# FFN down projections as seven products of sums of halves, on one Trainium2 core

## The chip, the cores and the metric

One core of a Trainium2 chip (trn2) runs the whole program. The metric is the device time of one execution in microseconds, as the median of several runs. The engines are called PE (TensorE), DVE (VectorE), ACT (ScalarE), POOL (GpSimd) and SP (SyncE, which here issues the loads).

## The reference

The reference applies two transformer layers and then a second block to x of 512 tokens and 1024 channels. The change is in the feed-forward part (FFN) of the two layers, and in where the second block's modulation vector is computed:

```python
def first_block(x, norm1, w_in, ..., norm2, w_up, w_down, final_norm):
    for l in range(DEPTH):                      # DEPTH = 2
        h = rms_norm(x, norm1[l])
        ...                                     # four kinds of attention, w_out
        h2 = rms_norm(x, norm2[l])
        x = x + jnp.square(jax.nn.relu(h2 @ w_up[l])) @ w_down[l]   # 1024 -> 4096 -> 1024
    return rms_norm(x, final_norm)

def second_block(x, c, norm_g, w_ada, b_ada, ...):
        mod = c @ w_ada[l] + b_ada[l]           # 1 x 1024 by 1024 x 3072
        shift, scale, gate = jnp.split(mod, 3, axis=-1)
        ...
```

## The kernel before

All matmuls are fp32 made of three products: each operand is split into a rounded part hi and a residue lo, and `mm3` (L159 to L161) adds hi·hi, hi·lo and lo·hi in one PSUM bank. Weights come through `send` (L118, a load of 512 KB into a ring `raw` of two buffers), `make` (L129: ACT copies to `whi`, L142, and DVE or POOL subtracts to `wlo`, L143, in rings of four) and `weights`, which makes two chunks more than are in use. `plan` lists the chunks in the order of use. The FFN's lo parts are made on DVE (`lo_engine`).

The FFN of a layer (`ffn`) runs over 8 column groups c of 512 hidden units. In each, four up tiles n (128 hidden units by 512 tokens, 24 matmuls each, here called U0 to U3) are computed by `feature_proj` into the two PSUM banks `acc`; ACT takes relu (L849) and the square's hi part (L850), POOL the square (L851), DVE its lo part (L852). Then the down projection takes the four tiles against four chunks of w_down: 8 PSUM tiles (4 token tiles by 2 halves of the columns, in `acc` and `sc` by turns) of 12 matmuls each, 96 in all, and DVE adds each to x (L869). A group has thus 96 + 96 matmuls of 128x512.

In groups 1 to 6 each up tile is followed by a piece of other work: in layer 0 a row block of w_ada_2 (a further load of 512 KB through the ring `raw`, which DVE multiplies by c and adds up, L952 and L954, with three small reductions on PE), in layer 1 a copy of bias rows for the second block (`bias_copy`). `bias_tables` stands ahead of group 5 of layer 0. The tile framework keeps the order of each engine's queue and adds the waits; a buffer of a ring is written again once its last reader is done.

Of the kernel before, what the change touches and what calls it, by code (L numbers as in the profile page):

```python
# [57 lines left out]
class Kern:  # L58
    def __init__(self, ctx, tc, t):
# [19 lines left out]
        self.raws, self.prepped = {}, {}  # L79
# [38 lines left out]
    def send(self):  # L118
        ap = self.plan[self.sent]
        kt, cols = ap.shape[1], ap.shape[2]  # L120
        raw = self.wp.tile([P, 1024], F32, tag="raw", name=self.name("raw"), bufs=RAWS)
        v = raw[:, : kt * cols].rearrange("p (k c) -> p k c", k=kt)
        self.nc.sync.dma_start(v, ap)
        self.raws[self.sent] = raw
        self.sent += 1

    def make(self):
        n = self.made
        while self.sent < min(len(self.plan), n + 3):  # L129
# [284 lines left out]

    def plan_layer(self, l):
# [14 lines left out]
        for what in ORDER:  # L430
# [20 lines left out]
            else:  # L451
                out("abcd".index(what))
        for c in range(8):
            for n in range(4):
                a = c * HALF + n * P
                plan.append(ch(t["w_up"][l, :, a : a + P]))
                if l == 0 and 4 * c + n in range(4, 28):
                    part, k = divmod(4 * c + n - 4, KD)
                    self.whole.add(len(self.plan) + len(plan))
                    plan.append(  # L460
                        ch(t["w_ada_2"][0, k * P : (k + 1) * P, part * D : (part + 1) * D])
                    )
            for half in range(2):
                for k in range(2):
                    a = c * HALF + k * 256
                    plan.append(
                        ch(t["w_down"][l, a : a + 256, half * HALF : (half + 1) * HALF])
                    )
# [362 lines left out]
    def ffn(self, l):  # L831
        nc = self.nc
        hT = self.norm_to_hT(self.row(self.t["norm2"][l]))
        for c in range(8):
            if l == 0 and c == 5:
                self.bias_tables()
            acts, ready = [], []
            for n in range(4):
                if c == 0 and n == 0:
                    ready = self.first_tiles(hT, self.weights(2))  # L840
                    self.lo_engine = nc.vector
                if ready:
# [10 lines left out]
                acts.append(a)  # L853
                if 4 * c + n in range(4, 28):
                    if l == 0:
                        self.modulation(*divmod(4 * c + n - 4, KD))
                    else:
                        self.bias_copy(4 * c + n - 4)

            def group(b, half, ws):  # L860
                out = self.psum(("acc", "sc")[b % 2])
                tok = slice(b * P, (b + 1) * P)
                for n, a in enumerate(acts):
                    w = ws[n // 2]
                    self.mm3(
                        out, (a[:, 0, tok], a[:, 1, tok]), (w[0][:, n % 2], w[1][:, n % 2]), n == 0, n == 3
                    )
                xs = self.x[:, b, half * HALF : (half + 1) * HALF]
                nc.vector.tensor_tensor(xs, out, xs, ALU.add)  # L869

            if c == 7:
                self.lo_engine = nc.gpsimd
                ws = self.weights(4)
                for b in range(NB):
                    for half in range(2):
                        group(b, half, ws[2 * half : 2 * half + 2])
            else:
                for half in range(2):
                    ws = self.weights(2)
                    for b in range(NB):  # L880
                        group(b, half, ws)

    def first(self):

        tc, t = self.tc, self.t
        with ExitStack() as es:
# [4 lines left out]
            for l in range(2):  # L891
# [4 lines left out]
                with ExitStack() as e2:  # L896
                    self.fp = e2.enter_context(tc.tile_pool(name=f"ffn{l}", bufs=1))
                    self.ffn(l)
                    if l == 0:
                        g = self.ffn_row(t["norm1"][1])  # L900
                        hT = self.norm_to_hT(g)
# [564 lines left out]
```

## Time and profile before

| | |
|---|---|
| median of 3 runs | 1921.62 us (1919.59 to 1922.48) |
| the profiled execution | 1929.24 us, its span 1927.1 us |
| granted PE clock over the span | 0.98 of full speed |
| busy share of the span | PE 95%, DVE 61%, ACT 44%, POOL 33% |
| FFN of layer 0 in the trace | about 322 to 686 us |
| FFN of layer 1 in the trace | about 1003 to 1348 us |

The span is the time from the first to the last instruction in one profiled execution, which here was longer than the median of the others; durations in the rows below are of this execution. A row of a timeline gives start, length, engine, line and operation, with the tile written and those read; "x2" joins two like operations in a row.

### The profile page before, as it was taken

The numbers are of one execution on the slowest core, as the hardware profiler recorded it, in microseconds if no ns is written. First come the engines' busy times: TensorE is split into PE (matmuls) and PEld (weight loads), VectorE is DVE, ScalarE is ACT, GpSimd is POOL, SyncE is SP. The second block draws the span as 40 slices with busy tenths as digits, with TensorE's granted clock in tenths as the row PEclk, the third lists the DMA queues.
The fourth block names the chain that finished last, engine by engine and source line by source line (L and its number), as shares of the span: only waits on it lengthen the run. The fifth ranks groups of instructions, "written<-read, shape, count | busy, mean of one in ns | idle before, by whom it ended". The sixth has DMA issues, their size and how long they took to land.

```text
span 1927.1 us, 25712 instructions
## 1 busy us (share of the span) xinstructions
PE 1825.6 (95%) x9414; PEld 1524.6 (79%) x9414; DVE 1172.1 (61%) x2376; ACT 850.6 (44%) x1842; POOL 628.5 (33%) x425
## 2 busy tenths in 40 slices
PE   7899998999999998999989999999798999999898
PEld 6788877888877887888768888888677887877677
DVE  5899666555545358997664443333748544559675
ACT  5656775332322246556753333322434343534323
POOL 3334343111111233343331111112346444433454
PEclk9999999999999999999999999999899999999999
DMA  4222112454465322211132333332332332322242
GB/s 152 67 83 61 45 48 80 131 153 143 134 180 158 94 57 67 79 46 54 55 98 83 101 92 97 99 99 87 98 101 64 95 99 66 88 61 78 66 148 98
DMA packets 220652, 178.51 MB, mean 93 GB/s; under 512 B 14735, under 2 KB 191279, under 8 KB 220527
## 3 DMA queue, kind: packets, MB, share of 16 engines
q1 hardware_dynamic: 220526, 176.88, 30.9%
q8 instruction: 74, 1.21, 0.3%
q14 instruction: 52, 0.42, 0.1%
HBM read 172.50 MB, written 8.03 MB: 94 GB/s over the span
## 4 chain that ended last, share of the span: by engine, by line
PE 77%; DVE 13%; DMA 4%; ACT 2%; issue 2%; POOL 1%; SPq 0%; ACTq 0%; DVEq 0%; POOLq 0%
PE acc L159 19%; PE acc L160 19%; PE acc L161 19%; PE sc L159 5%; PE sc L160 4%; PE sc L161 4%; PE tp L371 2%; DVE p L1213 1%; PE pv L302 1%; PE pv L303 1%; DVE b L1053 1%; DMA raw<-in_w_in_dram 1%; DMA nrow<-neg 1%; POOL wlo L143 1%; DVE dsa L568 1%
## 5 line engine op out<-in xcount | busy, mean ns | idle before, releaser
L142 ACT ACTIVATE whi<-raw 128x1024 fp32r<-128x1024 f32 (+6 forms) x288 | 289.4, 1005 | 620.4 <-PE acc L160 237.7
L143 POOL TENSOR_TENSOR wlo<-raw,whi 128x1024 fp32r<-128x1024 f32 (+7 forms) x172 | 377.3, 2200 | 445.7 <-ACT whi L142 411.3
L159 PE MATMUL acc<-hTh,whi 128*128 128x512 f32 (+1 forms) x1128 | 438.0, 390 | 12.2 <-DVE kz L167 4.6
L160 PE MATMUL acc<-hTl,whi 128*128 128x512 f32 (+1 forms) x1128 | 434.2, 385 | 2.5 <-DVE hTl L167 2.5
L161 PE MATMUL acc<-hTh,wlo 128*128 128x512 f32 (+1 forms) x1128 | 433.4, 385 | 0.0
L851 POOL TENSOR_TENSOR tmp<-tmp 128x512 f32<-128x512 f32 x64 | 103.0, 1610 | 567.9 <-ACT tmp L849 567.8
L159 PEld LDWEIGHTS acc<-hTh,whi 128*128 128x128 f32 x1128 | 214.9, 191 | 57.4 <-issue 7.0
L143 DVE TENSOR_TENSOR wlo<-raw,whi 128x1024 fp32r<-128x1024 f32 x116 | 142.8, 1231 | 176.5 <-ACT whi L142 176.5
L160 PEld LDWEIGHTS acc<-hTl,whi 128*128 128x128 f32 x1128 | 215.2, 191 | 41.6 <-DVE hTl L167 3.5
L161 PEld LDWEIGHTS acc<-hTh,wlo 128*128 128x128 f32 x1128 | 215.0, 191 | 40.2
L159 PE MATMUL acc<-whi,hTh 128*128 128x256 f32 (+3 forms) x512 | 158.5, 311 | 10.8 <-DVE t L280 5.3
L160 PE MATMUL acc<-wlo,hTh 128*128 128x256 f32 (+3 forms) x512 | 156.3, 306 | 1.4 <-POOL wlo L143 1.4
L161 PE MATMUL acc<-whi,hTl 128*128 128x256 f32 (+3 forms) x512 | 157.6, 308 | 0.1
L159 PEld LDWEIGHTS acc<-whi,hTh 128*128 128x128 f32 x512 | 99.8, 196 | 16.4 <-issue 4.8
L160 PEld LDWEIGHTS acc<-wlo,hTh 128*128 128x128 f32 x512 | 100.5, 196 | 4.5 <-POOL wlo L143 2.2
L159 PE MATMUL acc<-whi,act 128*128 128x512 f32 x256 | 99.6, 395 | 4.5 <-DVE x L869 4.3
L161 PEld LDWEIGHTS acc<-whi,hTl 128*128 128x128 f32 x512 | 100.1, 196 | 3.8 <-issue 1.9
L166 ACT ACTIVATE pt<-tp 128x512 fp32r<-128x512 f32 (+3 forms) x128 | 63.2, 513 | 89.3 <-PE tp L371 37.3
L160 PE MATMUL acc<-wlo,act 128*128 128x512 f32 x256 | 100.7, 393 | 0.0
L159 PE MATMUL sc<-whi,act 128*128 128x512 f32 x256 | 99.7, 389 | 0.0
L160 PE MATMUL sc<-wlo,act 128*128 128x512 f32 x256 | 99.7, 389 | 0.0
L161 PE MATMUL sc<-whi,act 128*128 128x512 f32 x256 | 99.3, 389 | 0.0
(333 smaller groups left out, 3591.7 us busy)
## 6 DMA issues: line engine op xcount, KB each, us to landing
raw<-in_w_in_dram SPq DMA_DIRECT2D x92, 512.0 KB, 4.0
raw<-in_w_up_dram SPq DMA_DIRECT2D x64, 512.0 KB, 4.1
raw<-in_w_down_dram SPq DMA_DIRECT2D x64, 512.0 KB, 3.5
raw<-in_w_out_dram SPq DMA_DIRECT2D x24, 512.0 KB, 3.4
raw<-in_w_ada_dram SPq DMA_DIRECT2D x24, 512.0 KB, 4.2
raw<-in_w_in_dram SPq DMA_DIRECT2D x8, 416.0 KB, 5.4
x<-in_x_dram SPq DMA_DIRECT2D x4, 512.0 KB
nrow<-neg SPq DMA_DIRECT2D x8, 256.0 KB, 4.2
```

What stands on the lines that cost most here:

```text
L142: self.nc.scalar.activation(hi, raw, AF.Copy)
L143: self.lo_engine.tensor_tensor(lo, raw, f(hi), ALU.subtract)
L159: mm(out, lhsT[0], rhs[0], start=first, stop=False)
L160: mm(out, lhsT[0], rhs[1], start=False, stop=False)
L161: mm(out, lhsT[1], rhs[0], start=False, stop=last)
L166: self.nc.scalar.activation(hi, src, AF.Copy)
L302: mm(out, both, th[0], start=first, stop=False)
L303: mm(out[0:64], v[:, j, x, 0], th[1], start=False, stop=False)
L371: nc.tensor.transpose(pt[:, at : at + P], hd["p"][:, src : src + P], self.ident)
L568: nc.vector.match_replace(out=a, in_to_replace=m8, in_values=a, imm_value=TAKEN)
L851: nc.gpsimd.tensor_tensor(r[:, S:], r[:, :S], r[:, :S], ALU.mult)
L1053: nc.vector.reciprocal(dst, dst)
```

## The change

Groups 0 to 4 of layer 0 and 0 to 6 of layer 1 (`SEVEN = (5, 7)`), 12 of 16, compute the down projection as a product of 2 x 2 blocks: A are the halves of the hidden tile (tokens by hidden units), B the four chunks of w_down, and seven products M1 to M7 of sums of blocks give the result. Each product has 2 token tiles by 2 blocks of 128 hidden units by 3 = 12 matmuls, 84 in all.

- Five of the seven weight operands are sums of two chunks: POOL makes them (L194, 128x1024, into the scratch ring `tmp` of three), ACT and DVE split them as before (L207, L208). The chunks are held in a ring `rawd` of five.
- The sums of hidden halves are made by POOL (L927, L933, L934 of 256 columns, L937 of 512), and each operand is split by ACT and DVE (`put`, L917 and L918). The square is now taken by DVE from PSUM (L981).
- M1 to M5 are added up over the groups in SBUF (L958, on DVE; ACT copies in group 0), and after the last seven-product group are added to x, M1 to M4 by POOL (L963, L964), M5 by DVE. M6 and M7 go to x at once (L952).
- Products of a group are spread: M3 and M6 after its own U2 and U3, M4 and M7, M1 and M2, and M5 after U0, U1 and U2 of the next group. The other groups stay as they were, but for the square.
- The 24 modulation rows stand two by two in groups 5 to 7 of layer 0. `bias_tables` moves to group 0 of layer 1, and the rows for the next norm are loaded ahead of the end of the FFN.

The diff, cut to its core:

```diff
+MADE = {
+    "M1": ("B11", "B22", ALU.add, "A11+A22"),
+    "M2": ("B11", None, None, "A21+A22"),
+    "M3": ("B12", "B22", ALU.subtract, "A11"),
+    "M4": ("B21", "B11", ALU.subtract, "A22"),
+    "M5": ("B22", None, None, "A11+A12"),
+    "M6": ("B11", "B12", ALU.add, "A21-A11"),
+    "M7": ("B21", "B22", ALU.add, "A12-A22"),
+}
...
+SEVEN = (5, 7)
+
+def after(l, c, n):
+    late = (("B21", "M4", "M7"), ("M1", "M2"), ("M5",), ())[n] if 0 < c <= SEVEN[l] else ()
+    early = ((), (), ("B12", "B22", "M3"), ("B11", "M6"))[n] if c < SEVEN[l] else ()
+    return late + early
...
+            _, one, two, op = e
+            raw, kt, cols = self.held[one], 2, HALF
+            if two:
+                both = self.scratch()
+                self.nc.gpsimd.tensor_tensor(both, raw, self.held[two], op)
+                raw = both
+            engine = self.nc.vector
...
+    def rows_of(self, l, c, n):
+        return [divmod(8 * (c - 5) + 2 * n + i, KD) for i in range(2)] if l == 0 and c >= 5 else []
...
+        def put(a, src):
+            nc.scalar.activation(a[:, 0], src, AF.Copy)
+            nc.vector.tensor_tensor(a[:, 1], src, f(a[:, 0]), ALU.subtract)
+
+        def hidden(c, n, s, sq):
+            g = nc.gpsimd.tensor_tensor
+            j = n % 2
+            if n < 2:
+                put(operand(c, ["A11"], j), s[:, :256])
+                t = self.half()[:, :256]
+                g(t, s[:, 256:], s[:, :256], ALU.subtract)
+                put(operand(c, ["A21-A11"], j), t)
+                return
+            s0 = sq[j]
+            put(operand(c, ["A22"], j), s[:, 256:])
+            t = self.half()
+            g(t[:, :256], s[:, :256], s[:, 256:], ALU.subtract)
+            g(t[:, 256:], s0[:, :256], s[:, 256:], ALU.add)
+            put(operand(c, ["A12-A22", "A11+A22"], j, "a4", S), t)
+            t = self.half()
+            g(t, s0, s, ALU.add)
+            put(operand(c, ["A11+A12", "A21+A22"], j, "a4", S), t)
+
+        def product(c, m):
+            (w,) = self.weights()
+            for t in range(2):
+                tok = slice(t * P, (t + 1) * P)
+                out = self.psum(("acc", "sc")[t])
+                for j in range(2):
+                    a = parts[c, MADE[m][3], j]
+                    self.mm3(out, (a[:, 0, tok], a[:, 1, tok]), (w[0][:, j], w[1][:, j]), j == 0, j == 1)
...
-                r = self.scratch()
-                nc.scalar.activation(r[:, :S], pj, AF.Relu)
-                nc.scalar.activation(a[:, 0], r[:, :S], AF.Square)
-                nc.gpsimd.tensor_tensor(r[:, S:], r[:, :S], r[:, :S], ALU.mult)
-                nc.vector.tensor_tensor(a[:, 1], r[:, S:], f(a[:, 0]), ALU.subtract)
+                    r = self.half()
+                    nc.scalar.activation(r, pj, AF.Relu)
+                    q = self.st.tile([P, S], F32, tag="sq", name=self.name("sq"), bufs=4)
+                    nc.vector.tensor_tensor(q, r, pj, ALU.mult)
+                    if c < SEVEN[l]:
+                        sq.append(q)
+                        hidden(c, n, q, sq)
...
+                    for part, k in self.rows_of(l, c, n):
+                        self.modulation(part, k)
+                    if l == 1 and c == 0 and n == 1:
+                        self.bias_tables()
...
```

The order of DVE's queue before, in layer 1, from the third residue of a group's weights to its down projection; `wlo` are residues of weights, `act` those of hidden tiles, `x` the evictions:

```order
L852 TENSOR_TENSOR act_1985_10253<-tmp_1986_10254,act_1985_10253 128x512
L852 TENSOR_TENSOR act_1987_10259<-tmp_1988_10260,act_1987_10259 128x512
L143 TENSOR_TENSOR wlo_2003_10342<-raw_1989_10265,whi_2002_10341 128x1024
L852 TENSOR_TENSOR act_1993_10296<-tmp_1994_10297,act_1993_10296 128x512
L143 TENSOR_TENSOR wlo_2006_10348<-raw_1995_10302,whi_2005_10347 128x1024
L852 TENSOR_TENSOR act_1999_10333<-tmp_2000_10334,act_1999_10333 128x512
L869 TENSOR_TENSOR x_84<-acc_2007_10351,x_84 128x512
L869 TENSOR_TENSOR x_84<-sc_2008_10365,x_84 128x512
L143 TENSOR_TENSOR wlo_2013_10410<-raw_2001_10339,whi_2012_10409 128x1024
L869 TENSOR_TENSOR x_84<-acc_2009_10379,x_84 128x512
L869 TENSOR_TENSOR x_84<-sc_2010_10393,x_84 128x512
L143 TENSOR_TENSOR wlo_2016_10416<-raw_2004_10345,whi_2015_10415 128x1024
```

DVE had eight weight residues, four hidden residues and eight evictions in a group, each reading what ACT, POOL or PE had left, in this order.

The order of DVE's queue in the changed kernel, in layer 1 from the square of U2 of group 3 to that of U3. `wlo_2372` belongs to U0 of the next group, `wlo_2384` to M4, `wlo_2389` to M7 (ahead of the fence stands `wlo_2368`, of M6); `sq_2354` and `sq_2375` are the squares of U2 and U3, `a2` and `a4` the operands made of hidden sums:

```order
L981 TENSOR_TENSOR sq_2354_11327<-t2_2353_11325,acc_2352_11300 128x512
L208 TENSOR_TENSOR wlo_2372_11391<-raw_2364_11364,whi_2371_11390 128x1024
L958 TENSOR_TENSOR M3_2208_10689<-sc_2370_11382,M3_2208_10689 128x512
L918 TENSOR_TENSOR a2_2355_11329<-sq_2354_11327,a2_2355_11329 128x256
L952 TENSOR_TENSOR x_84<-sc_2386_11454,x_84 128x512
L958 TENSOR_TENSOR M3_2206_10680<-acc_2369_11374,M3_2206_10680 128x512
L208 TENSOR_TENSOR wlo_2384_11443<-tmp_2382_11440,whi_2383_11442 128x1024
L918 TENSOR_TENSOR a4_2357_11335<-t2_2356_11332,a4_2357_11335 128x512
L918 TENSOR_TENSOR a4_2359_11340<-t2_2358_11338,a4_2359_11340 128x512
L208 TENSOR_TENSOR wlo_2389_11465<-tmp_2387_11462,whi_2388_11464 128x1024
L981 TENSOR_TENSOR sq_2375_11421<-t2_2374_11419,acc_2373_11394 128x512
```

The square, which frees the PSUM bank of an up tile, now stands behind residues of weight sums and of hidden sums, which read what POOL made.

The same queue, on to the square of U0 of the next group (`sq_2392`, read from `acc_2390`); `wlo_2397` belongs to U1, `wlo_2403` to M1, and `acc_2398` is the first tile of M4:

```order
L208 TENSOR_TENSOR wlo_2397_11507<-raw_2381_11438,whi_2396_11506 128x1024
L918 TENSOR_TENSOR a2_2376_11423<-sq_2375_11421,a2_2376_11423 128x256
L918 TENSOR_TENSOR a4_2378_11429<-t2_2377_11426,a4_2378_11429 128x512
L918 TENSOR_TENSOR a4_2380_11434<-t2_2379_11432,a4_2380_11434 128x512
L208 TENSOR_TENSOR wlo_2403_11531<-tmp_2401_11528,whi_2402_11530 128x1024
L958 TENSOR_TENSOR M4_2237_10817<-acc_2398_11510,M4_2237_10817 128x512
L981 TENSOR_TENSOR sq_2392_11495<-t2_2391_11493,acc_2390_11468 128x512
```

The square of U0 stands behind the residue of M1's weights and those of U3's three operands.

POOL's queue before holds only squares of hidden tiles in the FFN of layer 1 (L851), four in a group. In the changed kernel it goes as follows from the sum for M1 (`tmp_2401`) past U2 and U3 to the operands of U3; `tmp_2426` and `tmp_2443` are the sums for M3 and M6 of the next group:

```order
L194 TENSOR_TENSOR tmp_2401_11528<-rawd_2348_11292,rawd_2342_11268 128x1024
L933 TENSOR_TENSOR t2_2356_11332<-sq_2354_11327 128x256
L934 TENSOR_TENSOR t2_2356_11332<-sq_2315_11149,sq_2354_11327 128x256
L937 TENSOR_TENSOR t2_2358_11338<-sq_2315_11149,sq_2354_11327 128x512
L194 TENSOR_TENSOR tmp_2426_11640<-rawd_2414_11592,rawd_2419_11614 128x1024
L194 TENSOR_TENSOR tmp_2443_11714<-rawd_2425_11638,rawd_2414_11592 128x1024
L933 TENSOR_TENSOR t2_2377_11426<-sq_2375_11421 128x256
L934 TENSOR_TENSOR t2_2377_11426<-sq_2333_11235,sq_2375_11421 128x256
L937 TENSOR_TENSOR t2_2379_11432<-sq_2333_11235,sq_2375_11421 128x512
```

POOL's rows went from four to thirteen in a group, five of them of 128x1024, and each reads held chunks or squares that DVE makes.

The order of PE's queue in the changed kernel, between U3 and U0 of the next group; `sc_2399` belongs to M4, `sc_2405` to M7, `acc_2390` to U0, `acc_2385` to M6:

```order
L226 MATMUL acc_2385_11446<-whi_2367_11370,a2_2336_11242 128x512
L225 MATMUL sc_2399_11518<-wlo_2384_11443,a2_2355_11329 128x512
L226 MATMUL sc_2399_11518<-whi_2383_11442,a2_2355_11329 128x512
L224 MATMUL sc_2405_11542<-whi_2388_11464,a4_2357_11335 128x512
L225 MATMUL sc_2405_11542<-wlo_2389_11465,a4_2357_11335 128x512
L226 MATMUL sc_2405_11542<-whi_2388_11464,a4_2357_11335 128x512
L224 MATMUL acc_2390_11468<-hTh_2134_10336,whi_2371_11390 128x512
```

Matmuls of M4 and M7 now stand ahead of U0, so that U0 begins behind `wlo_2384` and `wlo_2389`. The tiles `acc` take their two banks by turns: `acc_2390` (U0) that of `acc_2373` (U3), and after `acc_2398` (M4) the second tile of M7, `acc_2404`, that of `acc_2390`.

## Rows read from the trace of the kernel before

**Rows 1.** The page: span; part 1: busy us, share of span, instructions by engine.
```profile
span 1927.1 us, 25712 instructions
...
PE 1825.6 (95%) x9414; PEld 1524.6 (79%) x9414; DVE 1172.1 (61%) x2376; ACT 850.6 (44%) x1842; POOL 628.5 (33%) x425
```

**Rows 2.** Windows, layer 1's FFN: busy us (instructions) by engine, granted clock.
```profile
1050.00:1093.00 43.00, 43.00 (x191) 35.63 (x190) 17.01 (x20) 12.96 (x16) 6.39 (x4) 1.00 0.32 95
```

**Rows 3.** Timeline of PE: first matmul of two groups of layer 1.
```profile
1054.47 0.39 PE L159 MATMUL acc<-hTh,whi 128*128 128x512 f32 x1
...
1097.99 0.39 PE L159 MATMUL acc<-hTh,whi 128*128 128x512 f32 x1
```

**Rows 4.** Timelines, layer 0's FFN; in brackets idle time before and its releaser.
```profile
550.12 0.47 PE L159 MATMUL acc<-hTh,whi 128*128 128x512 f32 x1 [0.85 <-DVE tb L991]
...
587.26 0.79 PE L159 MATMUL acc<-whi,act 128*128 128x512 f32 x1 [4.25 <-DVE x L869]
...
585.32 1.28 DVE L954 SCALAR_TENSOR_TENSOR ada<-raw,cvec,ada 128x1024 f32<-128x1024 f32 x1 [5.50 <-DMA raw<-in_w_ada_dram]
586.52 0.68 DVE L869 TENSOR_TENSOR x<-acc,x 128x512 f32<-128x512 f32 x1
```

**Rows 5.** Groups by form, 1050 to 1093: count, busy us, mean ns.
```profile
L142 ACT ACTIVATE whi<-raw 128x1024 fp32r<-128x1024 f32 x8 | 8.5, 1062 | 30.4 <-PE acc L160 14.3 <-PE sc L161 10.2 <-PE acc L161 6.0
...
L851 POOL TENSOR_TENSOR tmp<-tmp 128x512 f32<-128x512 f32 x4 | 6.4, 1596 | 37.5 <-ACT tmp L849 37.5
```

**Rows 6.** Timeline of DVE: three operations in a row.
```profile
587.72 1.21 DVE L143 TENSOR_TENSOR wlo<-raw,whi 128x1024 fp32r<-128x1024 f32 x1
588.85 0.68 DVE L869 TENSOR_TENSOR x<-acc,x 128x512 f32<-128x512 f32 x1
589.45 0.68 DVE L869 TENSOR_TENSOR x<-sc,x 128x512 f32<-128x512 f32 x1
```

**Rows 7.** Timelines of PE, ACT and DVE at an up tile's end.
```profile
431.31 0.39 PE L160 MATMUL acc<-hTl,whi 128*128 128x512 f32 x1
...
431.73 1.06 ACT L142 ACTIVATE whi<-raw 128x1024 fp32r<-128x1024 f32 x1 [2.23 <-PE acc L160]
432.70 0.58 ACT L849 ACTIVATE tmp<-acc 128x512 f32<-128x512 f32 x1
...
432.82 1.23 DVE L143 TENSOR_TENSOR wlo<-raw,whi 128x1024 fp32r<-128x1024 f32 x1 [1.57 <-ACT whi L142]
```

**Rows 8.** Timelines of POOL and DVE at three places where both work.
```profile
1357.83 5.28 POOL L143 TENSOR_TENSOR wlo<-raw,whi 128x1024 fp32r<-128x1024 f32 x2 [3.61 <-ACT whi L142]
...
1360.83 2.83 DVE L926 TENSOR_TENSOR nh<-x,row 128x512 f32<-128x512 f32 x1
...
1364.25 0.67 DVE L926 TENSOR_TENSOR nh<-x,row 128x512 f32<-128x512 f32 x1
...
315.43 4.66 POOL L143 TENSOR_TENSOR wlo<-raw,whi 128x1024 fp32r<-128x1024 f32 x2 [6.94 <-ACT whi L142]
...
317.72 0.68 DVE L412 TENSOR_TENSOR x<-sc,x 128x512 f32<-128x512 f32 x1
...
338.63 3.58 POOL L851 TENSOR_TENSOR tmp<-tmp 128x512 f32<-128x512 f32 x2 [18.54 <-ACT tmp L849]
...
339.53 1.77 DVE L143 TENSOR_TENSOR wlo<-raw,whi 128x1024 fp32r<-128x1024 f32 x1 [0.21 <-ACT whi L142]
```

**Rows 9.** Groups by form on POOL over the span.
```profile
L386 POOL TENSOR_TENSOR mix<-total,mix 64x512 fp32r<-64x512 f32 x32 | 41.6, 1300 | 67.1 <-ACT mix L385 66.4
...
L281 POOL TENSOR_TENSOR t<-t,t 128x256 f32<-128x256 f32 x24 | 18.4, 769 | 56.3 <-DVE t L280 42.7 <-DVE sa L335 5.8 <-PE tp L371 5.7
```

**Rows 10.** DMA issues: count, KB, median us from issue to landing.
```profile
raw<-in_w_up_dram SPq DMA_DIRECT2D x64, 512.0 KB, 4.1
...
raw<-in_w_ada_dram SPq DMA_DIRECT2D x24, 512.0 KB, 4.2
```

More of the change, by code (lines that the diff above doesn't have):

```diff
@@ L129, in make @@
         while self.sent < min(len(self.plan), n + 3):
-            self.send()
-        ap = self.plan[n]
+            if not self.send():
+                break
+        e = self.plan[n]
         self.made += 1
-        raw = self.raws.pop(n)
-        if n in self.whole:
-            self.prepped[n] = raw
+        if isinstance(e, tuple) and e[0] == "hold":
+            self.held[e[1]] = self.raws.pop(n)
             return
-        kt, cols = ap.shape[1], ap.shape[2]
+        self.ready_made += 1
+        engine = self.lo_engine
+        if isinstance(e, tuple):
+            _, one, two, op = e
[5 more added lines that the diff above has]
+            engine = self.nc.vector
+        else:
+            raw = self.raws.pop(n)
+            if n in self.whole:
+                self.prepped[self.ready_made - 1] = raw
+                return
+            kt, cols = e.shape[1], e.shape[2]
         m = kt * cols
@@ L452, in plan_layer, with up, down @@
                 out("abcd".index(what))
+        def up(c, n):
+            a = c * HALF + n * P
+            plan.append(ch(t["w_up"][l, :, a : a + P]))
+            for part, k in self.rows_of(l, c, n):
+                self.whole.add(len(self.plan) + len(plan))
+                plan.append(ch(t["w_ada_2"][0, k * P : (k + 1) * P, part * D : (part + 1) * D]))
+        def down(c, k, half):
+            a = c * HALF + k * 256
+            return ch(t["w_down"][l, a : a + 256, half * HALF : (half + 1) * HALF])
         for c in range(8):
             for n in range(4):
[L455 to L468, printed above, removed]
+                up(c, n)
+                for what in after(l, c, n):
+                    if what in PART:
+                        plan.append(("hold", what, down(c - (what == "B21"), *PART[what])))
+                    else:
+                        plan.append(("mix",) + MADE[what][:3])
+            if c >= SEVEN[l]:
+                plan += [down(c, k, half) for half in range(2) for k in range(2)]
         return plan
@@ new lines, in ffn, with operand @@
+        parts, sums = {}, {}
+        def operand(c, key, j, tag="a2", cols=256):
+            a = self.st.tile([P, 2, cols], F32R, tag=tag, name=self.name(tag), bufs=8 if tag == "a2" else 6)
+            for x in range(0, cols, 256):
+                parts[c, key[x // 256], j] = a[:, :, x : x + 256]
+            return a
+        def put(a, src):
[9 more added lines that the diff above has]
+                put(operand(c, ["A21-A11"], j), t)
+                return
+            s0 = sq[j]
[7 more added lines that the diff above has]
+            put(operand(c, ["A11+A12", "A21+A22"], j, "a4", S), t)
@@ L883, in first, with next_rows @@
+        self.st = None
+    def next_rows(self, l):
+        if l == 0:
+            self.rows = [self.row(self.t["norm1"][1])]
+        else:
+            self.rows = [self.ffn_row(r) for r in (self.t["final_norm"], self.mod[1], self.mod[0])]
     def first(self):
@@ L899, in first @@
                     if l == 0:
[L900 to L901 removed]
+                        hT = self.norm_to_hT(*self.rows)
                     else:
```

163 lines of the change are left out of this document (101 added, 62 removed).

## The prediction

> **What bounds the kernel now.** I read the share of each engine first: TensorE (PE) is busy 95% of the 1927.1 us span [rows 1], so a saving counts only where PE works without waiting. Then the windows: in a stretch of layer 1's FFN of 43.00 us, PE is busy 43.00, VectorE (DVE) 17.01, ScalarE (ACT) 12.96, GpSimd (POOL) 6.39, at a granted clock of 1.00, that is 2.4 GHz [rows 2]. Two groups start at 1054.47 and 1097.99 [rows 3]: 43.52 us for 192 products of 128x512, or 226.7 ns each. The FFN is PE's; the other engines have more than half their time free. Only two waits of PE stand out there, 0.85 us after the bias tables and 4.25 us where DVE's evictions were queued behind a modulation row that had itself waited 5.50 us for its load [rows 4]. Any product less is worth 226.7 ns as long as nothing else comes late. So the question is whether DVE, ACT and POOL can feed the new order.
>
> **What it removes.** A seven-product group has 84 down matmuls instead of 96. 12 x 12 groups x 226.7 ns = 32.6 us off PE. The 4.25 us wait goes with the modulation rows, which leave groups 1 to 6 [rows 4]; the 0.85 us moves along with the tables into layer 1 and is counted at nothing, since the same evictions wait for the same tables.
>
> **What it adds.** I take a frame, from the end of tile U2 of one group to that of the next (steady frames: 4 in layer 0, 6 in layer 1; and one at each end of the run of seven-product groups). PE has 180 products, 40.80 us. DVE has 11 weight residues (1.13 us from one start to the next), 14 evictions, 4 squares and 4 residues of 512 (0.60 each), and 6 residues of 256, for which I take 0.33, a straight line through 1.13 and 0.60 [rows 6]: 12.4 + 13.2 + 2.0 = 27.6 us. POOL has five weight sums at 2.33 (a pair took 4.66 [rows 8]), six sums of 256 at 0.77 and two of 512 at 1.30 [rows 9]: 18.9 us. ACT grows by 128x1024 copies of 1.06 [rows 5] and stays under 30 us. Each engine alone fits into 40.80. The price lies in how two of them meet.
>
> **DVE and POOL take turns.** POOL's pair that began at 1357.83 ended at 1363.11; a DVE operation with two SBUF operands that began at 1360.83 took 2.83 us, to 1363.66, where the same line took 0.67 once POOL was idle. But an eviction from PSUM took its usual 0.68 at 317.72, in the middle of a POOL pair that ran from 315.43 to 320.09. In the FFN it is there today: a weight residue took 1.77 us beside POOL's squares at 338.63 instead of 1.21 [rows 6, 8]. So I let a POOL operation and a DVE operation with two SBUF operands exclude each other for their whole length, and evictions and squares (one PSUM operand) run beside either. The Trainium skill has this as a rule that speaks against the change: "SBUF — State Buffer", section "SBUF: two separate sides", calls the shared port pair "an exclusive lock, not a bandwidth split", which the loser waits for during the whole instruction; the rows above agree. Exclusive work in a frame: 11 x 1.13 + 6 x 0.33 + 4 x 0.60 = 16.8 on DVE and 18.9 on POOL, 35.7 of 40.8 us. That fits on average; but it is a chain, since each waits for the other, for ACT, and for buffers that PE frees. Without the exclusion the sum would be the first rival's.
>
> **Chain A**, with t = 0 at the end of U2, names as in the fences above. The copy of M6's weights waits for a buffer that U2's products read (as 431.73 waits for 431.31, with the residue at 432.82 right behind [rows 7]): copy to 1.06, residue to 2.19. It frees the buffer of M1's weight sum on POOL: 2.33 to 4.66. Then in turns: residue of U0's weights to 5.79, POOL 256 to 6.56, DVE 256 to 6.89, POOL 256 to 7.66, POOL 512 to 8.96, residue of M4 to 10.09, DVE 512 to 10.69, POOL's sum for the next M3 (its buffer freed by M4's residue) to 13.02, DVE 512 to 13.62, residue of M7 to 14.75, square of U3 to 15.44. U0 takes U3's PSUM bank, so it can start at 15.5. PE alone would be there after 60 products, 13.60. Stall 1.9 us.
>
> **Chain B** goes on: POOL's sum for the next M6 (buffer freed by M7's residue) 14.85 to 17.18, residue of U1 18.31, POOL 256 19.08, DVE 256 19.41, POOL 256 20.18, POOL 512 21.48, two DVE 512 to 22.7. ACT, in its order, copies M1's weights at 22.1 to 23.1 (the buffer is U0's, whose products end at 20.9) and U0's relu behind it to 23.7, as at 431.73 and 432.70 [rows 7]; residue of M1 24.2, an eviction 24.8, square of U0 25.5. M7's second tile takes U0's bank and was due at 15.5 + 5.44 + 2.72 = 23.6. Stall 2.0 us. The rest of the frame (48 products of M1, M2, M5 and U1, U2) has slack, since only two POOL sums lie there.
>
> Period: 40.80 + 3.9 = 44.7 us against 43.52, 1.2 longer than before.
>
> **The ends of the run and the modulation.** In the frame from group 4 to 5 of layer 0, POOL adds four finished sums to x (1.30 each) in place of one weight sum, and DVE has two modulation rows of 1.2 (585.32 to 586.52 [rows 4]): A becomes 15.5 + 5.2 - 2.33 + 2.4 = 20.8, a stall of 7.2. B there: 2.0, 1.1 for a row ahead in DVE's order, and 2.7 for a row whose load is late, chosen midway between nothing and 4.2 + 1.28 [rows 4, 10]: 5.8. From 6 to 7 of layer 1 three such additions replace a sum: A 1.9 + 3.9 - 2.33 = 3.5, B 2.0.
> Groups 6 and 7 of layer 0 now send 16 loads each through a ring of two buffers. A weight chunk holds its buffer 4.1 + 1.06 + 1.23 = 6.4 us, a modulation row 4.2 + 1.28 = 5.5 [rows 4, 5, 7, 10]: (8 x 6.4 + 8 x 5.5)/2 = 47.6 us against 43.5. Group 5, 57 us long with 60 late products (43.5 + 13.6), lets the ring run ahead. Two groups x 4.1, half of it covered: +4, bounds 0 and 9. Nothing on POOL collides there, for it is idle but for the additions to x.
>
> **Sum.** -32.6 - 4.25; layer 0: A 4 x 1.9 + 7.2, B 4 x 2.0 + 5.8 = +28.6; layer 1: A 6 x 1.9 + 3.5, B 6 x 2.0 + 2.0 = +28.9; ring +4. Together **+24.7 us**. The profiled execution, 1929.24 with a span of 1927.1, becomes 1953.9 and 1951.8. The median of the runs, 1921.62, lies 7.6 lower, so I forecast **1946 us**. The measured runs lie 2.9 apart; 0.2% is 3.8 us and about what a measurement can tell from no change.
>
> **Rivals.**
> *The exclusion falls into slack (faster).* If POOL's operations land while DVE waits for ACT or PE anyway, chain B has only ACT's order left: U0 ends at 13.60 + 5.44 = 19.04, copy of M1 20.1, residue 21.2, eviction 21.8, square 22.5, against 21.76: 0.8, and 0.2 for A. 12 frames x 1.0 + 2 for the ends: -32.6 - 4.25 + 14 = -22.9, **1899 us**; with no stall at all 1885. For it: POOL's squares of 1.60 us today delay no product [rows 2, 5]. Against it: 35.7 of 40.8 us exclude each other. It decides where a steady frame's stalls fall under 1.44 us, as -32.6 - 4.25 + 4 + 18.5 (ends) + 10 x 1.44 = 0.
> *Everything on DVE and POOL is serial (slower).* If evictions too wait behind operations that wait for POOL, a frame takes 27.6 + 18.9 = 46.5, +3.0: 10 x 3.0 + 18.5 - 2 x 2.72 + 4 - 4.25 = +42.8, **1964 us**. For it: DVE works in order. Against it: 10.8 of DVE's 27.6 us read PSUM, and such an operation did not wait at 317.72 [rows 8].
> *The ring isn't covered (slower).* If each up tile of groups 6 and 7 waits for its three loads, it takes (6.4 + 2 x 5.5)/2 = 8.7 instead of 5.44: 8 x 3.3 = 26 in place of 4, **1968 us**. For it: the 5.50 us wait of today [rows 4]. Against it: the order puts several rows ahead, between evictions of the group before.
> That the products don't go away is excluded: the order has 12 matmuls for each of the seven.
>
> **How the numbers follow.** The forecast (1926 to 1962, from stalls half as long in every second frame to a full ring) has 0.46; a sum that comes out within 0.2%, with stalls of about 1.4 a frame, 0.08; exclusion in slack 0.27, no stall 0.05; serial 0.08; ring 0.06. Faster 0.32, same 0.08, slower 0.60. The range from 1897 to 1966 leaves out the no-stall case, half the ring's, and some of the tails.
>
> **What would show it.** In the profile after: layer 1's groups 44.7 us apart (40.8 if nothing waits); PE idle about 1.9 us before U0 and about 2.0 before M7's second tile, both ended by DVE's square at L981; POOL's sums at L194 well over 2.33 us on the mean and DVE's residues at L208 over 1.23; DVE and POOL together busy for most of the frame. I am wrong if PE's waits in a steady frame are under 1.44 us, or if they end on something else: a weight load, ACT's copies, the held raw blocks.

## The result, and the profile after

The changed kernel takes 1942.92 us (median of 4 runs, 1941.63 to 1944.37) against 1920.94 (4 runs, 1919.59 to 1922.48): ratio 1.0114, 95% interval 1.0097 to 1.0132, so 22 us slower. The forecast was 1946. The page of its profile, span and part 1, which answers to [rows 1]:

```profile
span 1941.8 us, 25881 instructions
...
PE 1807.4 (93%) x9270; PEld 1492.1 (77%) x9270; DVE 1428.6 (74%) x2610; ACT 923.8 (48%) x1970; POOL 850.8 (44%) x547
```

PE works 18 us less, DVE 256 and POOL 222 us more; a part of what these two have more is time in which one stood still for the other, as the rows below show. Where the span went is read from the windows of the stretches that end where the next norm's transposes or the next matmul phase begin: FFN of layer 0, attention of layer 1, FFN of layer 1. The columns are length, busy us of PE, its weight loads, DVE, ACT and POOL, the granted clock, DMA. First the changed kernel:

```profile
318.97:706.20 387.23, 358.58 (x1572) 289.66 (x1572) 300.14 (x326) 145.80 (x213) 151.31 (x85) 0.97 0.39 116
706.20:1009.82 303.62, 284.34 (x1775) 242.85 (x1774) 240.29 (x678) 193.61 (x501) 121.17 (x95) 1.00 0.23 67
1009.82:1372.53 362.71, 347.54 (x1528) 280.10 (x1529) 297.89 (x322) 155.97 (x232) 197.01 (x112) 0.98 0.35 105
```

The same three stretches of the kernel before:

```profile
321.80:690.38 368.58, 363.13 (x1636) 299.39 (x1637) 187.04 (x229) 114.59 (x163) 61.54 (x36) 0.98 0.45 132
690.38:1003.70 313.32, 291.03 (x1776) 249.35 (x1774) 243.65 (x675) 194.32 (x496) 123.83 (x96) 0.97 0.23 67
1003.70:1359.55 355.85, 355.15 (x1608) 295.71 (x1609) 148.85 (x188) 112.18 (x158) 59.20 (x37) 0.99 0.31 95
```

The FFNs take 387.23 + 362.71 us against 368.58 + 355.85, 25.5 more, and the forecast's sum for them was 24.7. The attention between them, whose code is the same, takes 9.7 less, at a clock of 1.00 against 0.97; the spans differ by 14.7 and the medians by 22.0, for the profiled execution of before lay 8 us above its median.

PE's timeline in the changed kernel, one row for each wait of which the text speaks, and U0 of two groups in a row (1141.49, 1184.89), which answer to [rows 3]:

```profile
339.14 0.47 PE L224 MATMUL acc<-hTh,whi 128*128 128x512 f32 x1 [2.86 <-DVE sq L981]
...
533.76 0.76 PE L224 MATMUL sc<-whi,a 128*128 128x512 f32 x1 [4.48 <-DVE x L952]
...
576.34 0.50 PE L225 MATMUL sc<-wlo,a 128*128 128x512 f32 x1 [3.44 <-DVE wlo L208]
...
647.09 0.50 PE L224 MATMUL acc<-whi,a 128*128 128x512 f32 x1 [3.55 <-DVE x L1009]
...
1028.96 0.50 PE L224 MATMUL sc<-whi,a 128*128 128x512 f32 x1 [1.90 <-ACT a L917]
...
1141.49 0.50 PE L224 MATMUL acc<-hTh,whi 128*128 128x512 f32 x1
...
1184.29 0.50 PE L225 MATMUL sc<-wlo,a 128*128 128x512 f32 x1 [1.08 <-DVE wlo L208]
...
1184.89 0.50 PE L224 MATMUL acc<-hTh,whi 128*128 128x512 f32 x1
...
1194.11 0.50 PE L224 MATMUL acc<-whi,a 128*128 128x512 f32 x1 [0.77 <-DVE M L958]
```

A steady frame takes 43.40 us. 180 products are 40.80, so 2.6 are lost: two waits of 1.08 and 0.77, and 0.75 in the slower starts of the matmuls around them. Before, a group took 43.52. Twelve products less in a group buy 0.12 us.

DVE's timeline in the changed kernel:

```profile
338.32 0.67 DVE L981 TENSOR_TENSOR sq<-t,acc 128x512 f32<-128x512 f32 x1
...
644.01 1.28 DVE L1102 SCALAR_TENSOR_TENSOR ada<-raw,cvec,ada 128x1024 f32<-128x1024 f32 x1 [3.67 <-DMA raw<-in_w_ada_dram]
...
1171.03 1.23 DVE L208 TENSOR_TENSOR wlo<-tmp,whi 128x1024 fp32r<-128x1024 f32 x1 [2.43 <-ACT whi L207]
...
1172.77 0.68 DVE L981 TENSOR_TENSOR sq<-t,acc 128x512 f32<-128x512 f32 x1
...
1173.36 2.46 DVE L208 TENSOR_TENSOR wlo<-raw,whi 128x1024 fp32r<-128x1024 f32 x1
...
1179.61 3.49 DVE L918 TENSOR_TENSOR a<-t,a 128x512 fp32r<-128x512 f32 x2
...
1184.16 0.68 DVE L981 TENSOR_TENSOR sq<-t,acc 128x512 f32<-128x512 f32 x1
...
1193.37 0.68 DVE L958 TENSOR_TENSOR M<-acc,M 128x512 f32<-128x512 f32 x1
...
1193.97 0.68 DVE L981 TENSOR_TENSOR sq<-t,acc 128x512 f32<-128x512 f32 x1
```

POOL's:

```profile
326.88 10.43 POOL L194 TENSOR_TENSOR tmp<-rawd,rawd 128x1024 f32<-128x1024 f32 x4 [10.78 <-PE tp L330]
...
1172.33 2.40 POOL L194 TENSOR_TENSOR tmp<-rawd,rawd 128x1024 f32<-128x1024 f32 x1 [6.68 <-DVE wlo L208]
...
1174.70 1.72 POOL L933 TENSOR_TENSOR t<-sq 128x256 f32<-128x256 f32 x1
...
1179.77 2.78 POOL L194 TENSOR_TENSOR tmp<-rawd,rawd 128x1024 f32<-128x1024 f32 x1 [1.16 <-DVE wlo L208]
```

At 1173.36 a residue takes 2.46 us, since POOL's sum runs from 1172.33 to 1174.73; POOL's 256 columns of 1174.70 then take 1.72, since that residue runs to 1175.82; at 1179.61 two residues of hidden sums take 3.49 beside the sum of 1179.77, where one takes 0.60. Turns, as in [rows 8], and U0 follows the square of 1184.16.

Beyond the products that went or moved (226.7 ns each), the starts of U0 in the two timelines give for each part of the FFNs:

| part | before us | after us | products | beyond them | forecast |
|---|---|---|---|---|---|
| layer 0, norm to group 1 | 49.62 | 38.20 | -72 | +4.9 | |
| groups 1 to 3 | 131.56 | 129.17 | -36 | +5.8 | with the line above 13.6 |
| group 4 | 47.14 | 49.95 | -12 | +5.5 | |
| groups 5 to 7 | 140.26 | 169.91 | +60 | +16.1 | with the line above 14.75 |
| layer 1, norm to group 1 | 50.77 | 45.88 | -66 | +10.1 | |
| groups 1 to 6 | 261.12 | 260.50 | -72 | +15.7 | |
| group 7 | 43.96 | 56.33 | +54 | +0.1 | layer 1: 28.9 |

The wait of chain A lies ahead of U0 and that of chain B behind it, so the 2.0 of the last steady frame's chain B in layer 0 stand in the line of group 4.

### The profile page after: what moved, and what is told of

It reads as the page before. It is cut to its first block, busy times and chain, and to the rows that moved or that the text cites. A ratio compares the mean times of both kernels' runs of the same rounds, so it can differ in the third digit from the quotient of the medians.

```text
span 1941.8 us, 25881 instructions
## 1 busy us (share of the span) xinstructions
PE 1807.4 (93%) x9270; PEld 1492.1 (77%) x9270; DVE 1428.6 (74%) x2610; ACT 923.8 (48%) x1970; POOL 850.8 (44%) x547
## 5 line engine op out<-in xcount | busy, mean ns | idle before, releaser
L208 POOL TENSOR_TENSOR wlo<-raw,whi 128x1024 fp32r<-128x1024 f32 (+4 forms) x170 | 372.7, 2198 | 549.6 <-ACT whi L207 509.5
L224 PE MATMUL acc<-hTh,whi 128*128 128x512 f32 (+1 forms) x1128 | 443.1, 394 | 16.8 <-DVE sq L981 6.6
L207 ACT ACTIVATE whi<-raw 128x1024 fp32r<-128x1024 f32 (+6 forms) x240 | 238.4, 994 | 304.6 <-PE acc L225 111.1
L225 PEld LDWEIGHTS acc<-hTl,whi 128*128 128x128 f32 x1128 | 217.5, 193 | 42.4 <-DVE hTl L232 3.3
L194 POOL TENSOR_TENSOR tmp<-rawd,rawd 128x1024 f32<-128x1024 f32 x60 | 150.8, 2516 | 166.4 <-DVE wlo L208 91.1
L208 DVE TENSOR_TENSOR wlo<-raw,whi 128x1024 fp32r<-128x1024 f32 x70 | 115.0, 1643 | 29.8 <-ACT whi L207 29.6
L225 PE MATMUL sc<-wlo,a 128*128 128x512 f32 x232 | 93.0, 401 | 15.7 <-DVE wlo L208 15.7
L207 ACT ACTIVATE whi<-tmp 128x1024 fp32r<-128x1024 f32 x60 | 63.5, 1058 | 89.3 <-PE acc L225 61.3
L208 DVE TENSOR_TENSOR wlo<-tmp,whi 128x1024 fp32r<-128x1024 f32 x60 | 84.1, 1401 | 27.7 <-ACT whi L207 27.6
L224 PE MATMUL acc<-whi,a 128*128 128x512 f32 x232 | 91.8, 396 | 12.5 <-DVE M L958 6.1
L224 PE MATMUL sc<-whi,a 128*128 128x512 f32 x232 | 91.2, 394 | 7.9 <-DVE x L952 5.4
```

The source lines that it names most:

```text
L194: self.nc.gpsimd.tensor_tensor(both, raw, self.held[two], op)
L207: self.nc.scalar.activation(hi, raw, AF.Copy)
L224: mm(out, lhsT[0], rhs[0], start=first, stop=False)
L225: mm(out, lhsT[0], rhs[1], start=False, stop=False)
```

## The experiments

Ratios are to the kernel before, run on the same chip; "the changed kernel" is the one above.

**1. Weight sums on DVE.**

```diff
-                self.nc.gpsimd.tensor_tensor(both, raw, self.held[two], op)
+                self.nc.vector.tensor_tensor(both, raw, self.held[two], op)
```

> The five weight sums of a group (128x1024) are made by DVE instead of POOL; everything else as in the changed kernel. Theory (POOL and two-operand DVE work exclude each other, and that chain makes the waits of PE): exclusive work falls from 16.8 + 18.9 = 35.7 to 16.8 + 5.65 + 7.2 = 29.7 us a frame; the two waits of a steady frame, which cost 2.64 us of 43.40 in the changed kernel, fall to between 0 and 1.4, so the frame takes 40.8 to 42.2 us; with the first group's wait of 2.86 gone too the time is about 1921 us (1915 to 1932). Rival (DVE's own load and its order of work make the waits): DVE gets 5 x 1.13 us more, the frame stays at 43.4 or grows, 1943 to 1955 us.

1931.83 us, ratio 1.0041 (1.0028 to 1.0054). PE's timeline, U0 of two groups of layer 1 that lie two apart:

```profile
1133.77 0.50 PE L224 MATMUL acc<-hTh,whi 128*128 128x512 f32 x1
...
1217.10 0.50 PE L224 MATMUL acc<-hTh,whi 128*128 128x512 f32 x1
```

41.67 us a frame: as the theory said, though DVE has 5.65 us more to do. The time is at the upper end of its range, because layer 0 (380.9 us) gained only 6.

**2. Hidden sums on DVE as well.**

```diff
-            g = nc.gpsimd.tensor_tensor
+            g = nc.vector.tensor_tensor
```

> As the run before, and the eight hidden sums of a group on DVE too: POOL does nothing in a frame, DVE has 27.6 + 5.65 + 6 x 0.33 + 2 x 0.6 = 36.4 us of 40.8. Theory (exclusion): no operation waits for the other engine, the frame takes 40.8 to 41.6 us and the time is 1912 to 1925 us, not above the run before by more than 3. Rival (DVE's load): the queue of DVE is 89% full and its evictions come late, the frame takes over 43.4 us, 1945 us or more.

1935.50 us, ratio 1.0057 (1.0039 to 1.0076), frames of 42.4 us. The theory missed here: with no exclusion left in the frame it is 0.7 longer than in run 1, and the wait of PE that is left (0.55 us, at 1178.70) ends on a residue of DVE. So DVE's own work or order seems to be the limit by then, but not by as much as the rival said; which of the two was not taken apart.

**3. Fills in place of sums.** The weight sums are left out; POOL fills the buffer twice.

```diff
-                self.nc.gpsimd.tensor_tensor(both, raw, self.held[two], op)
+                for v in (0.25, 0.5):
+                    self.nc.gpsimd.memset(both, v)
```

> POOL writes each of the five weight sums by two fills with a constant, which read nothing from SBUF, instead of adding two chunks; so the sums are left out, but POOL still writes the buffers that ACT and DVE read, in the same places of its order, and DVE's operations are those of the changed kernel. Theory (two-operand work of DVE and POOL operations that read SBUF exclude each other): the steady frame falls from 43.40 us to 41.7 or less, DVE's weight residues lie at 1.2 to 1.3 us again where a fill runs beside them, 1915 to 1928 us. Rival (it is only the time that POOL takes for a sum, or DVE's order): with two fills of about 0.95 us the frame stays over 42.8 us, 1936 us or more.

1930.56 us, ratio 1.0040 (1.0024 to 1.0056), 2.6 above the theory's range and below the rival's. PE's timeline, U0 of two groups in a row:

```profile
1130.65 0.50 PE L225 MATMUL acc<-hTh,whi 128*128 128x512 f32 x1
...
1172.27 0.50 PE L225 MATMUL acc<-hTh,whi 128*128 128x512 f32 x1
```

41.62 us, under the theory's bound. Two fills take 1.97 where a sum takes 2.40, and three sums lie in chains A and B, so the shorter time alone would give 43.40 - 3 x 0.43 = 42.1; the frame tells the theories apart by 0.5 us only. What tells them apart clearly are the operations side by side. POOL's timeline:

```profile
1160.80 1.97 POOL L195 MEMSET tmp<- 128x1024 f32 x2 [7.17 <-DVE wlo L209]
...
1167.01 1.97 POOL L195 MEMSET tmp<- 128x1024 f32 x2 [1.14 <-DVE wlo L209]
```

DVE's:

```profile
1161.86 1.22 DVE L209 TENSOR_TENSOR wlo<-raw,whi 128x1024 fp32r<-128x1024 f32 x1
...
1166.87 1.28 DVE L919 TENSOR_TENSOR a<-t,a 128x512 fp32r<-128x512 f32 x2
```

A residue of 1.22 and two of 0.64 each, beside fills that run to 1162.77 and 1168.98; beside sums the same places of the changed kernel read 2.46 and 3.49. Fills read nothing and block nothing. The Trainium skill, "SBUF — State Buffer", section "SBUF: two separate sides", says so of the lock: against a DVE operation with two SBUF inputs it counts only for a GpSimd operation that reads SBUF. These rows agree.

**4. The change without seven products.**

```diff
-SEVEN = (5, 7)
+SEVEN = (0, 0)
```

> No group uses seven products; all 16 down projections are direct, and the other moves of the change stay: the modulation rows two by two in groups 5 to 7, the bias tables in layer 1, the square on DVE from PSUM. Theory (the trace after: groups 5 to 7 cost some 10 us more with two rows a tile): 1926 to 1935 us, with the last three groups of layer 0 at 47 to 52 us each. Rival (the prediction's step: the ring costs 4 and the wait of 4.25 us goes): 1917 to 1925 us.

1943.44 us, ratio 1.0107 (1.0081 to 1.0133). No product less, no sum on POOL, and the time is that of the changed kernel. It is over both ranges. PE's timeline in groups 5 and 6 of layer 0:

```profile
590.26 0.79 PE L224 MATMUL acc<-whi,a 128*128 128x512 f32 x1 [5.59 <-DVE x L1009]
...
642.87 0.80 PE L224 MATMUL acc<-whi,a 128*128 128x512 f32 x1 [5.62 <-DVE x L1009]
```

DVE's, ahead of the first of them:

```profile
587.19 1.28 DVE L1102 SCALAR_TENSOR_TENSOR ada<-raw,cvec,ada 128x1024 f32<-128x1024 f32 x1 [3.67 <-DMA raw<-in_w_ada_dram]
...
589.52 0.68 DVE L1009 TENSOR_TENSOR x<-acc,x 128x512 f32<-128x512 f32 x1
```

A modulation row waits 3.67 us for its load, and the evictions behind it in DVE's order come when PE has stood still for 5.59.

**5. The same, with the modulation rows in groups 1 to 6.**

```diff
-        return [divmod(8 * (c - 5) + 2 * n + i, KD) for i in range(2)] if l == 0 and c >= 5 else []
+        return [divmod(4 * c + n - 4, KD)] if l == 0 and 4 * c + n in range(4, 28) else []
```

> No seven products, and the modulation rows one by one in groups 1 to 6 of layer 0; what is left of the change are the bias tables in layer 1, the square on DVE, and the rows of the next norm loaded early. Theory (two rows a tile in three groups cost 12 us or more; the tables at the head of layer 1's FFN about 5 us net; the square on DVE 0.4 us a group): 1926 to 1933 us. Rival (the tables or the square carry most of the 20 us of the kernel without seven products): 1937 us or more.

1923.35 us, ratio 1.0002 (0.9989 to 1.0015): the time of the kernel before, though its parts differ (layer 0's FFN is 5.9 us shorter than before, layer 1's, with the tables at its head, 8.6 longer). Layer 0's FFN, run 4 and below it this run, each from its own windows:

```profile
319.91:702.72 382.81, 366.88 (x1633) 301.42 (x1633) 202.39 (x257) 113.39 (x157) 8.68 (x4) 0.97 0.40 119
```

```profile
318.34:680.98 362.64, 360.30 (x1632) 297.36 (x1632) 202.67 (x257) 113.53 (x157) 8.84 (x4) 0.99 0.42 125
```

20.2 us lie in layer 0's FFN, as much as the medians differ by (20.1). That is the price of two rows a tile in three groups when nothing else is changed.

**6. The changed kernel with its rows in groups 1 to 6** (the edit of run 5 alone).

> The 24 modulation rows stand where they stood before the change, one behind each up tile of groups 1 to 6 of layer 0; the rest as in the changed kernel. Theory (the end groups pay for two rows a tile, about 10 us in all; a row is a further two-operand operation of 1.2 us in DVE's exclusive work, 35.7 + 4.9 of 40.8 us in a steady frame): groups 5 to 7 give back 8 to 10 us, the four steady frames of layer 0 lose 2.4 to 3 us each, about 1945 us (1938 to 1952). Rival (rows cost only where two follow one tile): 1931 to 1936 us.

1958.78 us, ratio 1.0186 (1.0155 to 1.0217), layer 0's FFN 401.2 us: 7 us over the upper bound. The rows cannot go back either: in a seven-product frame a row is a further two-operand operation in the chain between POOL and PE, and waits of 1.8 to 4.9 us stand in the groups from 1 on.

**7. A ring of their own for the rows of groups 6 and 7.**

```diff
+        if self.sent in self.far:
+            raw = self.st.tile([P, 1024], F32, tag="rawd", name=self.name("rawd"), bufs=5)
+        else:
+            raw = self.wp.tile([P, 1024], F32, tag="raw", name=self.name("raw"), bufs=RAWS)
```

> The 16 modulation rows of groups 6 and 7 are loaded into the ring of five held chunks, which is idle by then, instead of the ring of two; the rest as in the changed kernel. Theory (evictions and squares on DVE stand behind modulation rows whose loads wait for the ring of two): the waits of 2.15, 3.55 and 1.55 us in groups 6 and 7 go, with the lower clock behind them 6 to 10 us, 1932 to 1938 us. Rival (DVE's work or its order is too long there, not the loads): 1941 us or more.

1941.21 us, ratio 1.0096 (1.0073 to 1.0119), in the rival's range. The three waits went, as the theory said, and layer 0's FFN took 382.0 us in place of 387.2; but the median is only 1.7 lower, which the runs cannot tell from the changed kernel. In groups 6 and 7 the ring is a part, about 5 us, no more; the rows of group 5 stayed in the ring of two, and what it costs there no run shows.

**8. Bias tables back in layer 0.** `bias_tables` stands ahead of group 5 again, in the changed kernel.

> The changed kernel with the bias tables back ahead of group 5 of layer 0. Theory (their place is a small part: at the head of layer 1's FFN they cost about 4 us, 354.5 us of FFN with them and 350.1 without in the two runs with the sums on DVE, and in layer 0 they cost 3 to 7): 1940 to 1947 us, layer 1's FFN near 358 us. Rival (moving them carries a large part of the loss): 1936 us or less.

1952.69 us, ratio 1.0149 (1.0122 to 1.0176), over both. Layer 1's FFN fell from 362.7 to 357.0, as expected, but in layer 0 PE waited for the tables' input, whose load SP issued at 530.97, behind two modulation rows that had held its queue for 8.06 us:

```profile
534.55 1.02 PE L1137 MATMUL acc<-tmp,t 33*24 33x512 f32 x1 [6.16 <-DMA t<-in_rel_bias_dram]
```

**9 and 10. Seven products in layer 1 alone, sums on DVE, rows in groups 1 to 6**, tables ahead of group 5 of layer 0, then ahead of group 7.

```diff
-SEVEN = (5, 7)
+SEVEN = (0, 7)
...
-                if l == 0 and c == 5:
+                if l == 0 and c == 7:
                     self.bias_tables()
```

> Seven products in groups 0 to 6 of layer 1 alone, their weight sums on DVE; layer 0 direct, its modulation rows in groups 1 to 6 and the bias tables ahead of group 5, as before the change. Theory (layer 1's frame is 41.7 us against 43.52 with the sums on DVE; no ring or tables in the way): layer 0 some 3 us longer for the square, layer 1 8 us shorter, 1912 to 1919 us, below the kernel before. Rival (the head of the run of seven-product groups costs what they save): 1921 us or more.

> The kernel with seven products in layer 1 alone and sums on DVE, with the bias tables ahead of group 7 of layer 0, behind the last modulation row, instead of ahead of group 5. Theory (the waits of 1.30 and 3.21 us in groups 5 and 6 come from the tables in the queues that the rows also use): layer 0's FFN falls from 370.4 to about 366 us, the time to 1909 to 1914 us. Rival (the tables cost the same at any place): 1915 us or more.

1915.79 us, ratio 0.9966 (0.9952 to 0.9980), and 1910.01, ratio 0.9923 (0.9899 to 0.9948): 13 us below the kernel before. The windows of the second, as above:

```profile
320.55:685.64 365.09, 361.98 (x1636) 297.08 (x1636) 203.55 (x260) 113.52 (x157) 8.85 (x4) 0.99 0.46 135
685.64:988.09 302.45, 284.44 (x1775) 242.86 (x1773) 240.35 (x678) 194.43 (x501) 121.54 (x95) 1.00 0.23 68
988.09:1338.20 350.11, 342.91 (x1528) 279.86 (x1528) 293.34 (x354) 154.02 (x232) 115.27 (x77) 0.99 0.32 97
```

Layer 1's FFN is 5.7 us shorter than before, layer 0's 3.5. That makes 9.2 of the 13; layer 0 has no seven products here, and no run has the tables late with direct products alone, so the 13 are not the price of the seven products.

**11. The square on POOL in the direct groups.**

```diff
+                        nc.scalar.activation(a[:, 0], r, AF.Square)
+                        nc.gpsimd.tensor_tensor(q, r, r, ALU.mult)
+                        nc.vector.tensor_tensor(a[:, 1], q, f(a[:, 0]), ALU.subtract)
```

> As the run before, and the direct groups take their square as before the change: ACT the rounded square, POOL the square, DVE the residue. Theory (the square on DVE lets ACT's copy wait for DVE and costs 0.36 us a group, 43.88 against 43.52): nine direct groups, some 3 us less, 1906 to 1911 us. Rival (POOL's square excludes DVE's residues as much as it helps): no change, 1909 to 1914 us.

1917.61 us, ratio 0.9962 (0.9948 to 0.9976), slower than run 10. Layer 0's FFN gave the 3.5 us (361.6), but layer 1's took 354.3, with a new wait of 2.53 in its last, direct group, and the attention 309.8 at a lower clock. Inconclusive for the square alone.

**12. The kernel before again**, one execution.

> The kernel before, unchanged, for a second profile. In the first one the stretch from layer 0's FFN to the norm of layer 1's FFN took 313.3 us, with a granted clock of 0.61 at 820 to 830 us, against 303 to 306 us in the kernels tried so far, whose code is the same there. If the low clock was that one execution's, the stretch takes 302 to 307 us here, the span is near 1919 us, and the whole difference of the two kernels lies in the two FFNs; if it belongs to the kernel, 311 us or more.

1924.64 us, span 1922.5, the stretch 310.7 us: just between the two expectations. The two FFNs took 369.0 and 356.1, as in the first profile.

## Why the prediction was right, point by point

**PE bounds the FFN, 32.6 us of products go.** Right: a frame is 40.80 us of products and the waits.

**POOL and DVE take turns, and chains A and B delay U0 and M7's second tile.** The rows of the changed kernel show that operations of POOL and DVE wait for each other, and those of run 3 that DVE's do not wait for a POOL operation that reads nothing. Run 1 alone does not tell the turns from POOL's longer sum (2.40 us, on DVE 1.30), and in run 3 the shorter operations could give 1.3 of the 1.8 us that the frame lost. So the turns are shown; how much of the 2.6 us is theirs is not. From M6's residue (1171.03) to U0 (1184.89) it takes 13.86 us where the working has 14.4. The size was off: 2.6 a frame, not 3.9. A costs 1.5 with the slow starts (forecast 1.9), since several operations of the chain were a little shorter than taken. B costs 1.1 (forecast 2.0), mostly because the step "M7's second tile takes U0's bank" failed: it began at 1194.11, 0.06 behind the eviction of M4's tile (1193.37 to 1194.05) and ahead of the end of U0's square, so its bank is M4's. The signs named ahead came out in part: the groups are 43.40 apart and not 44.7, and PE's two waits end on M7's residue (L208), with U0 0.05 behind U3's square, and on M4's eviction (L958), not both on a square; in the frame from 1141.49 POOL's sums have a mean of 2.46 us, hardly over the 2.33, and DVE's residues one of 1.54, well over 1.23.

**Groups 4 to 7 of layer 0.** The step that was mis-sized most. The working had 2.0 + 13.0 + 4 - 4.25 = 14.75 beyond the products, the trace has 21.6. Its mechanism, rows that wait for loads ahead of evictions, is in the rows at 644.01 and 647.09, and runs 4 and 5 give the rows' move 20.2 us in a kernel without seven products. Run 7 leaves only 5 us of the changed kernel's loss to the ring in groups 6 and 7; groups 4 and 5 have waits of 4.48 (533.76), 2.40 (548.57) and 3.44 (576.34) in which the additions to x, the modulation rows and residues of weights stand in one queue. DVE's timeline ahead of them:

```profile
530.73 2.28 DVE L1102 SCALAR_TENSOR_TENSOR ada<-raw,cvec,ada 128x1024 f32<-128x1024 f32 x1
...
545.50 1.28 DVE L1102 SCALAR_TENSOR_TENSOR ada<-raw,cvec,ada 128x1024 f32<-128x1024 f32 x1 [3.47 <-DMA raw<-in_w_ada_dram]
...
568.33 2.36 DVE L1102 SCALAR_TENSOR_TENSOR ada<-raw,cvec,ada 128x1024 f32<-128x1024 f32 x1
...
574.00 2.28 DVE L208 TENSOR_TENSOR wlo<-raw,whi 128x1024 fp32r<-128x1024 f32 x1
```

POOL's additions to x:

```profile
526.32 7.82 POOL L963 TENSOR_TENSOR x<-x,M 128x512 f32<-128x512 f32 x4
...
564.46 10.75 POOL L963 TENSOR_TENSOR x<-x,M 128x512 f32<-128x512 f32 x6 [1.76 <-DVE M L958]
```

One row waits 3.47 us for its load, but the other two and the residue take about 2.3 us in place of 1.28 and 1.21, beside POOL's additions. The working had four additions in chain A and let the twelve of group 5 collide with nothing: that term was missing. How much of the three waits is due to each was not separated.

**Not in the working: the heads of the runs.** 4.9 us in layer 0, where U2 waited 2.86 for a square (338.32) behind a residue beside POOL's four sums that began at 326.88, and 10.1 in layer 1, where M3 stands ahead of U2 and waits 1.90 for an operand (1028.96), and the tables' four matmuls follow; run 8 without the tables there took 5.7 less. From 1029.82 to 1044.82 the granted clock was 0.62, 0.50 and 0.85 in slices of 5 us, which makes some 5 of the 10.1.

**Not in the working: the clock behind a wait.** In slices of 5 us, (1 - granted clock) x time adds up to 18.1 us in the FFNs of the changed kernel and 8.0 before. Two such slices of the changed kernel, behind the waits of 533.76 and 647.09 (the granted clock is the third value from the end):

```profile
534.00:539.00 5.00, 4.25 (x10) 2.97 (x11) 5.00 (x5) 1.05 (x2) 3.24 (x4) 0.50 0.42 110
645.00:650.00 5.00, 2.91 (x13) 2.42 (x14) 3.83 (x6) 0.58 (x1) 0.00 (x0) 1.00 0.63 208
```

The first is at the lower level, 1.2 GHz, the second at 2.4. So up to 10 of the 25.5 us are not waits but the half clock that followed them.

So the sum for the FFNs, 24.7 against 25.5, holds out of terms that missed by -2.9 (layer 0's head and groups 1 to 3), +6.9 (groups 4 to 7) and -3.0 (layer 1, where the head missed by +8.2 and the rest by -11.2). The direction and the mechanism were right; that the sum came within 1 us is luck. The 9.7 us that the attention took less (7.1 against the second profile of before) stood in no term; the low clock went with them (9.4 us of (1 - granted clock) x time before, 8.0 in the second profile, 0 after), and why it fell stays open. The rival in which the exclusion falls into slack is refuted by a steady loss of 2.6 us, over the 1.44 that was named. The serial rival is refuted too: the square of 1172.77 took 0.68 beside POOL's sum of 1172.33. The price of the ring in full, 26 us, is nearer to the 20.2 of runs 4 and 5 than the 4 that was taken, though the ring is only a part of the loss in the changed kernel (run 7).

Taken apart by runs: without seven products, rows in groups 1 to 6, ratio 1.0002; rows moved, 1.0107; seven products, rows not moved, 1.0186; both, 1.0114. With the rows moved the seven products bought nothing. The rows' move cost 20 us without seven products and saved 14 (1.0186 to 1.0114) with them, so the two cannot be added up; with seven products in layer 0 the rows are dear at either place.

Layer 1's FFN shows the seven products by themselves, for runs 5 and 1 both have the tables at its head and the square on DVE. Run 5 with direct products, below it run 1 with seven products and their sums on DVE:

```profile
983.18:1347.60 364.42, 361.41 (x1617) 297.23 (x1618) 170.79 (x225) 112.46 (x158) 10.14 (x5) 0.99 0.35 103
```

```profile
1005.45:1359.98 354.53, 348.15 (x1532) 281.30 (x1532) 295.58 (x357) 153.71 (x232) 113.96 (x77) 0.98 0.36 107
```

Of the 19.0 us of products that go in seven groups, 9.9 are won; with the sums on POOL (362.71 in the changed kernel) it is 1.7. Run 4, whose layer 1 has the code of run 5, took 366.64, so both are good to some 2 us.

## What to carry to other kernels

Here twelve matmuls fewer in a group, 2.72 us, bought 0.12 us with the operands' sums on POOL and 1.85 with them on DVE. So where both engines work on two SBUF operands, count this work of DVE and POOL as that of one engine and follow it as a chain, not as a share. Moved work is priced by what stands behind it in an engine's queue: with a row of 1.28 us that waited for its load ahead of evictions, PE stood still for 5.59. Try the parts of a change alone, for here some of them together (seven products in layer 1, sums on DVE, tables late) made the kernel 13 us faster, and the whole made it 22 slower.

## What the runs showed of the hardware

The low clock moves. With the same code the attention of layer 1 took 301.6 to 306.2 us in ten of the kernels with the changed code, 309.8 and 312.7 in two, and 313.3 and 310.7 in two executions of the kernel before; (1 - clock) x time in it was 0 to 3.4, 5.8, 7.9, 9.4 and 8.0 us. In the first profile of before, a wait of 2.00 us at 760.21 left the clock at 1.00 from 760 to 770, and one of 1.94 us at 817.10 was followed by 0.61 from 820 to 830; in the changed kernel the wait of 3.55 us at 647.09 left it at 1.00, and behind that of 4.48 us at 533.76 it was 0.50, the lower of its two levels, from 534 to 539. What PE did before does not tell them apart in these rows. So a difference under some 8 us between two profiles should not be read without the column of the clock.
